# Queries and keys of a hybrid decoder layer moved ahead of attention, as seven block products per pair of heads

## The chip, the cores and the metric

One core of a Trainium2 chip runs the whole layer as one program. The metric is device time in microseconds (us); lower is better. A core has a matrix engine (PE, with its weight loads as PEld), a vector engine (DVE), a scalar engine (ACT), a general engine (POOL) and a queue engine (SP) that issues most transfers. Each takes its own instructions strictly in order.

## The reference

Everything is float32; 1024 tokens, model width 1024, one layer. Cut to what the change touches:

```python
h = rms_norm(x, attn_norm_w)
q, k, v, u, g = jnp.split(h @ w_in, splits, axis=-1)
q = rms_norm(q.reshape(B, S, 8, 2, 64), q_norm_w)      # per head two halves of 64
k = rms_norm(k.reshape(B, S, 8, 2, 64), k_norm_w)
a = diff_attention(q1, q2, k1, k2, v, lam, rel_bias)   # softmax(q1 k1) - lam * softmax(q2 k2), causal
y_a = (rms_norm(a, subln_w) * (1 - lam_init)) @ w_proj_attn
c = causal_depthwise_conv(u_a * sigmoid(u_b), conv_w, conv_b)      # width 31, 1024 channels
y_b = silu(layer_norm(c)) @ w_proj_conv
x = x + (sigmoid(g_a) * y_a + sigmoid(g_b) * y_b) @ w_out
x = x + (silu(gate) * up) @ w_down                     # from rms_norm(x) @ w_gate_up, width 2816
```

## The kernel before, in words

A float32 product is made of three products of rounded parts: each operand is split into a high part (`whi`, cast by ACT, L120) and a low part (`wlo`, a subtraction, on DVE at L125 or on POOL at L131, as the flag `low_by_pool` says), and PE runs high by high, high by low and low by high (L168 to L170).

The program runs in stages, and PE is the engine that nearly always works. After the norm of x and its transposes (`hT`), the values V1, V2 and the first columns of u are made. Then u follows in pairs of column blocks by **seven products** (`u_pair`, `product` at L980): with sums T1 to T4 of the blocks of `hT`, and sums of the weight blocks (`s`, L961 to L964 on POOL), seven block products replace eight. Behind these run the **taps** of the depthwise convolution, 30 for each of eight blocks of 128 channels, each one DVE instruction (L594) on a row of 1024 tokens; the first four blocks' sums lie in PSUM (`CONV_PSUM = 4`), the last four in SBUF. Next come Q0 and V3, and then attention.

**q and k before.** `q_item(h)` multiplies `hT` with the q and k columns of one head, plainly: 192 matmuls of 256 columns. ACT copies the result (L797) and squares it with 16 short instructions per 1024 columns that add up (L800); roots follow, and DVE multiplies them in (L807). Then `turn_qk` turns it: four transposes on PE (`pQ`, L815), a cast by ACT (L822), a low part by DVE (L824), and transfers within SBUF on SP, six for q (L826 to L832) and two for k (L836, L837). Q0 is made before attention, Q1 to Q7 inside it.

**Attention** has 64 steps: eight heads, in each eight tiles of 128 queries in the order 4, 5, 6, 7, 0, 1, 2, 3. A step makes two score rows on PE (`sc`, L1289 with the low keys or queries at L1290), DVE adds the bias and takes the maximum (L1291), ACT takes the exponential (L1296), DVE combines both (L1303 to L1306). One step later the weights are transposed (`pT`, L1328, "turn") and split, and for every second tile multiplied with the values (`pW`, "weigh"), two steps after that turned back. So that PE has work while the others run, each step takes a piece of other products as **fill**: the lists `later` name Q1 to Q7 and the gates G0 to G15 by head, a piece being 48 matmuls of 256 or 24 of 512 columns (5.4 to 5.8 us). Taps left over are handed to DVE by `slack_of`, which gives each step's spare time as two formulas of the tile size. The order of each engine's instructions is set while the program is recorded: a scheduler places them by their dependences and the marks `issue_after`.

**After attention** come y_a, the convolution branch, w_out, and the channel mixer, which the change does not touch.

## Time and profile before

| what | number |
|---|---|
| time, median of 3 runs (lowest to highest) | 1727.1 us (1726.74 to 1728.84) |
| profiled execution: span from first to last instruction | 1725.7 us, 1.4 us under that median |
| instructions | 25863 |
| PE busy | 1714.6 us, 99% of the span |
| DVE, ACT, POOL busy | 1275.4, 862.5, 219.1 us |
| u by seven products (110 to 247) | 137 us |
| Q0 and V3 (247 to 306) | 59 us |
| attention with its fill (306 to 817) | 511 us |

No time of the profiled execution is given beside its span; what lies around it is taken as the 1.4 us by which the median of the runs is longer. In the rows of groups, a line number, an engine, an operation and its tiles come first (`out<-in`), then the count, the busy time, the mean of one in ns, and the idle time of the engine ahead of them with what ended it. In the rows of windows, each engine has busy time and count, then comes the granted clock of PE.

### The profile page before, as it was taken

Reading aid. Unit: us, or ns where it says so; the run is one execution under the profiler, and the core shown is the slowest. Engines: PE = TensorE matmul, PEld = TensorE weight load, DVE = VectorE, ACT = ScalarE, POOL = GpSimd, SP = SyncE. Lnnn points to the kernel's source line nnn. Section 1 sums busy time; section 2 is a strip of 40 time slices with the busy share of each in tenths; the row PEclk is TensorE's granted clock in tenths of the full one; section 3 lists DMA queues with packets and bytes.
Section 4 is the critical chain, followed back from the end, with each engine's and each line's share of the span. In section 5 each row is a group of like instructions: output and inputs, shape, how many; then the busy total and the mean of one; then the engine's idle time right before and its main releaser. Section 6 shows DMA issues by size and latency. Waiting matters only on the chain.

```text
span 1725.7 us, 25863 instructions
## 1 busy us (share of the span) xinstructions
PE 1714.6 (99%) x9243; PEld 1477.9 (86%) x9243; DVE 1275.4 (74%) x2128; ACT 862.5 (50%) x1958; POOL 219.1 (13%) x207
## 2 busy tenths in 40 slices
PE   9999999999999999999999999999999999999999
PEld 7997889998998998988788888888888888888887
DVE  7675889898988888878687769966676666575544
ACT  5333335767777776756556325633333333333332
POOL 3997851000000000000000000000000000000000
PEclk9999999999999999999999999999999999999999
DMA  6344445336345344343973683245455445598663
GB/s 208 116 126 132 131 151 154 104 109 171 104 127 147 115 125 138 101 136 130 333 238 118 200 296 119 74 135 164 147 170 170 154 141 164 175 355 285 217 215 130
DMA packets 261604, 281.64 MB, mean 163 GB/s; under 512 B 16546, under 2 KB 181986, under 8 KB 261475
## 3 DMA queue, kind: packets, MB, share of 16 engines
q1 hardware_dynamic: 254160, 267.71, 48.3%
q0 software_dynamic: 5680, 9.39, 2.6%
q10 hardware_dynamic: 1634, 2.89, 0.5%
q8 instruction: 73, 1.20, 0.3%
q14 instruction: 57, 0.46, 0.1%
HBM read 181.84 MB, written 85.50 MB: 155 GB/s over the span
## 4 chain that ended last, share of the span: by engine, by line
PE 92%; DMA 3%; DVE 2%; ACT 1%; issue 1%; POOL 0%; SPq 0%; DVEq 0%; POOLq 0%; ACTq 0%
PE acc L980 29%; PE acc L488 12%; PE pg L168 12%; PE pg L169 12%; PE pg L170 12%; PE wo L1850 3%; PE sc L1290 2%; PE sc L1289 2%; PE pT L1328 2%; PE pg L1106 1%; DVE acc L594 1%; PE pW L168 1%; PE pW L169 1%; PE pW L170 1%; PE pQ L815 1%
## 5 line engine op out<-in xcount | busy, mean ns | idle before, releaser
L594 DVE SCALAR_TENSOR_TENSOR acc<-u,cw,acc 128x1023 f32<-128x1023 f32 (+14 forms) x240 | 303.4, 1264 | 23.2 <-ACT acc L588 20.7
L170 PE MATMUL pg<-whi,hT_lo 128*128 128x256 f32 x704 | 200.2, 285 | 0.0
L168 PE MATMUL pg<-whi,hT_hi 128*128 128x256 f32 x704 | 199.7, 285 | 0.4 <-DVE v L125 0.4
L169 PE MATMUL pg<-wlo,hT_hi 128*128 128x256 f32 x704 | 199.5, 284 | 0.0
L125 DVE TENSOR_TENSOR wlo<-draw,whi 128x1024 fp32r<-128x1024 f32 x75 | 91.7, 1223 | 83.4 <-ACT whi L120 78.9
L120 ACT CAST whi<-draw 128x1024 fp32r<-128x1024 f32 x75 | 79.1, 1055 | 129.5 <-PE acc L488 114.3
L169 PEld LDWEIGHTS pg<-wlo,hT_hi 128*128 128x128 f32 x704 | 134.4, 191 | 1.8
L170 PEld LDWEIGHTS pg<-whi,hT_lo 128*128 128x128 f32 x704 | 134.3, 191 | 1.8
L168 PEld LDWEIGHTS pg<-whi,hT_hi 128*128 128x128 f32 x704 | 134.0, 191 | 2.1 <-DVE v L125 0.6
L120 ACT CAST whi<-wraw 128x1024 fp32r<-128x1024 f32 x90 | 94.7, 1052 | 70.6 <-PE pg L169 32.6
L488 PE MATMUL acc<-wlo,whi 128*128 128x512 f32 x308 | 119.8, 389 | 0.0
L488 PE MATMUL acc<-whi,wlo 128*128 128x512 f32 x308 | 119.8, 389 | 0.0
L1296 ACT ACTIVATE E<-E,mn 128x640 f32<-128x640 f32 (+7 forms) x128 | 99.8, 781 | 30.8 <-DVE mn L1291 29.2
L168 PE MATMUL pg<-hT_hi,whi 128*128 128x512 f32 x288 | 114.4, 397 | 0.1
L169 PE MATMUL pg<-hT_lo,whi 128*128 128x512 f32 x288 | 113.7, 395 | 0.0
L170 PE MATMUL pg<-hT_hi,wlo 128*128 128x512 f32 x288 | 113.7, 395 | 0.0
L120 ACT CAST whi<-s 128x1024 fp32r<-128x1024 f32 x54 | 56.9, 1053 | 104.9 <-PE acc L980 101.8
L125 DVE TENSOR_TENSOR wlo<-wraw,whi 128x1024 fp32r<-128x1024 f32 x75 | 93.3, 1246 | 12.6 <-ACT whi L120 12.3
L1291 DVE CUSTOM_DVE_ANT_0 E<-sc,tb 128x512 f32<-128x512 f32 (+3 forms) x128 | 74.2, 585 | 33.2 <-PE pT L1328 16.1
L980 PE MATMUL acc<-h_hi,whi 128*128 128x512 f32 x240 | 93.4, 389 | 0.0
L980 PE MATMUL acc<-h_lo,whi 128*128 128x512 f32 x240 | 93.4, 389 | 0.0
L980 PE MATMUL acc<-h_hi,wlo 128*128 128x512 f32 x240 | 90.1, 389 | 0.0
(370 smaller groups left out, 4589.7 us busy)
## 6 DMA issues: line engine op xcount, KB each, us to landing
wraw<-in_w_gate_up_dram SPq DMA_DIRECT2D x44, 512.0 KB, 4.7
wraw<-in_w_in_dram SPq DMA_DIRECT2D x38, 512.0 KB, 4.0
qs<-qs SPq DMA_DIRECT2D x96, 128.0 KB, 2.3
wd<-in_w_down_dram SPq DMA_DIRECT2D x44, 256.0 KB, 3.1
tdT<-wd SPq DMA_DIRECT2D x88, 128.0 KB, 4.8
draw<-sdS SPq DMA_DIRECT2D x44, 256.0 KB, 3.7
draw<-tdT SPq DMA_DIRECT2D x44, 256.0 KB, 3.7
wraw<-in_w_in_dram SPq DMA_DIRECT2D x32, 256.0 KB, 3.3
```

The source lines that it names most:

```text
L120: act.copy(dst, src)
L125: last_lo[0] = dve.tensor_tensor(dst, src, f32(hi), op=ALU.subtract).ins
L168: pe.matmul(o, lh, rh, start=start, stop=False)
L169: pe.matmul(o, lh, rl, start=False, stop=False)
L170: last_mm[0] = pe.matmul(o, ll, rh, start=False, stop=stop).ins
L488: m = pe.matmul(o[s_][i][:], l_[:, ts], r_[:, 512:], start=start and j + y_ == 0, stop=j == n - 1 and y_ == 2, skip_group_check=not start,)
L594: dve.scalar_tensor_tensor(a_, us[c][:, : S - n], cw[:, c, t : t + 1], a_, op0=ALU.mult, op1=ALU.add)
L980: last_mm[0] = pe.matmul(o[:], a_[x_][:, k, :], b_[y_][:, k, :], start=start and k + x_ + y_ == 0, stop=k == 3 and x_ == 1, skip_group_che ...
L1289: pe.matmul(o[:, :w], qh[:, qs], k, start=True, stop=False)
L1291: dve.tensor_tensor_reduce(e[:, ks], o[:, :w], tb[:, S - nk + c0 : S - nk + c0 + w], 1.0, mn[:, j : j + 1] if c0 else 3.0e38, ALU.add, ALU ...
L1296: act.activation(e[:, :nk], e[:, :nk], AF.Exp, bias=mn[:, j : j + 1], scale=-1.0, accum_out=l[:, j : j + 1])
L1850: last_mm[0] = pe.matmul(o[s_][i][:], A[u_], B[v_], start=start and j + y_ == 0, stop=j == 3 and y_ == 2, skip_group_check=not start,).ins
```

## The change

**q and k.** A new stage, `q_stage`, stands between the last u pair and V3. It makes q and k of all eight heads, two heads at a time, by the seven products of `QSEVEN`, with the same token sums T1 to T4 and with sums and differences of the four weight blocks of a pair (`S1` to `S4`). A product is 48 matmuls of 256 columns, a pair 336, all four pairs 1344. The parts of a result are copied (`take`, ACT), added (`plus`, DVE) and, when complete, stored to memory (`qk_d`), squared 512 columns at a time by ACT and summed by a DVE reduction (`keep`). The roots of six heads are taken at once ahead of the last pair, those of the last two before V3 (`qk_roots`, DVE). Weight sums and low parts are POOL's, but for the first pair, where DVE makes two differences, one sum and one low part.

**In attention** nothing of Q is left; q and k are loaded again (`qk_load`, two transfers of 512 KB a head on SP), multiplied with their roots by POOL (`qk_norm`; DVE for head 0) and turned as before, at places named by `free`. The fill is G0 to G15 alone, in pieces of 6 matmuls of 512 columns, one between a step's two score rows (`amid`) and one behind them. A turn is two steps behind its scores instead of one, and values are weighed a step behind the turn. There are six places for score rows (`e_tile`) instead of four. `low_by_pool` stays set through attention, and POOL also multiplies in the norm of the attention output, but for the last head (`subln`).

**Convolution.** Six blocks' sums lie in PSUM, and all but 63 of the items (taps and transfers) of the list are done when attention starts, where 127 were left before. Signs and scales of the norms move into the constants `qn` and `kn`.

```diff
+    wplace = [cycle((1, 2, 0))]
+
     def wtiles():
-        return [wp.tile([P, 1024], F32R, tag=t_, name=nm(t_)) for t_ in ("whi", "wlo")]
+        z = next(wplace[0])
+        return [wp.tile([P, 1024], F32R, tag=f"{t_}{z}", name=nm(t_), bufs=1) for t_ in ("whi", "wlo")]
...
-    last = ["Q0", "V3"]
-    later = [
-        ["Q1", "G0", "G1"],
-        ["Q2", "G2", "G3"],
-        ["Q3", "G4"],
-        ["Q4", "G5", "G6"],
-        ["Q5", "G7"],
-        ["Q6", "G8", "G9"],
-        ["Q7", "G10"],
-        ["G11", "G12", "G13", "G14"],
-        ["G15"],
-    ]
+    last = ["V3"]
+    later = [f"G{c}" for c in range(2 * NKT)]
...
-    CONV_PSUM = 4
+    CONV_PSUM = 6
+    rs = cv.tile([P, 2 * H * 16], F32, tag="rs", name="rs", bufs=1)
...
-            o = gemm_T(w, hT_hi, hT_lo, sb)
+            o = pg()
+            cs = slice(sb * 512, (sb + 1) * 512)
+            for k in range(NKT):
+                mm3(o[:], w[0][:, k, :], w[1][:, k, :], hT_hi[:, k, cs], hT_lo[:, k, cs], k == 0, k == NKT - 1)
+                if k % 2 and k < NKT - 1:
+                    yield
...
+    def qk_load(h, b):
+        raw = qkp.tile([P, 4, 256], F32, tag="qkraw", name=f"qkraw{h}_{b}", bufs=2)
+        nc.sync.dma_start(raw[:].rearrange("p i c -> p (i c)"), qk_d[h][b][:])
+        return raw
+
+    def qk_roots(h0, h1):
+
...
+    def qk_norm(h, b, raw):
+
+        r = rs[:, 32 * h + 16 * b : 32 * h + 16 * b + 16]
+        r4 = raw[:].rearrange("p i (g d) -> p (i g) d", d=HD)
+        (pool if h else dve).tensor_tensor(r4, r4, r.unsqueeze(2).to_broadcast([P, 16, HD]), op=ALU.mult)
+        for z, key in ((1, "k"), (0, "q")):
+            free = NT * (h - 1) + (0 if key == "k" and b else NT - 1 if key == "q" and not b else NT // 2 - 1)
+            late.append((free if h else 0, lambda a_=(h, z, key, b, raw): turn_qk(*a_)))
+
+    def turn_qk(h, z, key, b, raw):
...
+            lo2 = part(4)
+            for one, two in ((s1, s2), (lo, lo2)):
+                if one is lo:
+                    dma(f32(two[HD:, :]), f32(one[HD:, :]))
+                dma(f32(two[:HD, :]), f32(one[HD:, :]))
+                dma(f32(one[HD:, :]), f32(one[:HD, :]))
+            t["q", b] = (s1, lo), (s2, lo2)
...
+    QSEVEN = (
+        ("11", (0, 0), "b"),
+        ("12", (1, 0), "a"),
+        ("S2", 2, "b"),
+        ("S1", 1, "c"),
+        ("S3", 3, "b"),
+        ("S4", (1, 1), "c"),
+        ("22", 4, "b"),
+    )
+    RATE = [3.25]
+    first_q = {}
...
+    def q_pair(c, load):
+
+        B = {(j, l): (hT_hi[:, KH[j], TOK[l]], hT_lo[:, KH[j], TOK[l]]) for j in range(2) for l in range(2)}
+        B.update(TS)
+        tags = ((ps, "pg"), (pg2, "pg2"), (ps, "pm"))
+        o = {}
+        for s_, r in (("b", c), ("a", c + 1), ("c", c + 2)):
+            p_, tag = tags[r % 3]
+            o[s_] = [p_.tile([P, 512], F32, tag=tag, name=nm("qo")) for e in range(2)]
+        seen, out = set(), {}
+        A = dict(first_q) if c == 0 else load.pop("A")
+        raw = load.pop("raw")
+
+        def less(o_, a_, b_, op=ALU.subtract, eng=pool):
...
+            eng.tensor_tensor(o_[:], a_[:], b_[:], op=op)
...
+        def take(k, s_):
+            t_ = quarter(k)
+            for e in range(2):
+                act.copy(t_[:, 2 * e : 2 * e + 2, :].rearrange("p i c -> p (i c)"), o[s_][e][:])
+
+        def plus(k, s_):
+            for e in range(2):
+                t_ = out[k][:, 2 * e : 2 * e + 2, :].rearrange("p i c -> p (i c)")
+                dve.tensor_tensor(t_, o[s_][e][:], t_, op=ALU.add)
+
+        def keep(k):
+            h, b = 2 * c + k[0], k[1]
+            t_ = out[k]
+            nc.sync.dma_start(qk_d[h][b][:], t_[:].rearrange("p i c -> p (i c)"))
+            for e in range(2):
+                jk = wp.tile([P, 512], F32, tag="sg", name=nm("qsq"), bufs=2)
+                act.activation(jk[:], t_[:, 2 * e : 2 * e + 2, :].rearrange("p i c -> p (i c)"), AF.Square)
+                c0 = 32 * h + 16 * b + 8 * e
+                dve.tensor_reduce(
+                    rs[:, c0 : c0 + 8], jk[:].rearrange("p (g d) -> p g d", d=HD), axis=AX.X, op=ALU.add
+                )
+
+        for z, (a_, b_, s_) in enumerate(QSEVEN):
+            hi_lo = A.pop(a_)
+            Bz = B[b_]
+            for i in range(4):
+                ts = slice(i * P, (i + 1) * P)
+                e, w = i // 2, slice(256 * (i % 2), 256 * (i % 2 + 1))
+                for k in range(4):
+                    for x_, y_ in ((0, 0), (0, 1), (1, 0)):
+                        last_mm[0] = pe.matmul(
+                            o[s_][e][:, w], Bz[x_][:, k, ts], hi_lo[y_][:, k, :],
+                            start=s_ not in seen and i % 2 == 0 and k + x_ + y_ == 0, stop=k == 3 and x_ == 1,
+                            skip_group_check=True,
+                        ).ins
+            seen.add(s_)
+            if z == 0:
+                take((0, 0), "b")
+                if c == 0:
+                    less(raw["S1"], raw["21"], raw["22"], ALU.add, dve)
+                    less(raw["21"], raw["11"], raw["21"], eng=dve)
+                less(raw["11"], raw["S1"], raw["11"], eng=pool if c else dve)
+                low_by_pool[0] = c > 0
+                A["S2"] = q_split(raw["11"])
+                low_by_pool[0] = True
+            elif z == 1:
+                plus((0, 0), "a")
+                keep((0, 0))
+                A["S1"] = q_split(raw["S1"])
+            elif z == 2:
+                take((0, 1), "b")
+                A["S3"] = q_split(raw["21"])
+                less(raw["12"], raw["12"], raw["11"])
+            elif z == 3:
+                take((1, 1), "c")
+                A["S4"] = q_split(raw["12"])
+                load(c, "11", "21")
+            elif z == 4:
+                plus((1, 1), "b")
+                keep((1, 1))
+                A["22"] = q_split(raw["22"])
+                load(c, "12", "22")
+            elif z == 5:
+                plus((0, 1), "c")
+                keep((0, 1))
+                load(c, "split 11")
+            else:
+                take((1, 0), "b")
+                keep((1, 0))
+                load(c, "split 12", "sums")
+            yield
...
+        def __call__(self, c, *what):
+            raw, A = self.have.setdefault("raw", {}), self.have.setdefault("A", {})
+            for w in what:
+                if c == H // 2 - 1:
+                    if w[:5] == "split":
+                        ws.ahead = int(w == "split 12")
+                        ws.fetch()
+                elif w == "sums":
+                    raw["S1"] = self.tile("S1")
+                    pool.tensor_tensor(raw["S1"][:], raw["21"][:], raw["22"][:], op=ALU.add)
+                    pool.tensor_tensor(raw["21"][:], raw["11"][:], raw["21"][:], op=ALU.subtract)
+                elif w[:5] == "split":
+                    A[w[6:]] = q_split(raw[w[6:]])
+                else:
+                    raw[w] = self.tile(w)
+                    q_load(raw[w], 2 * (c + 1) + int(w[0] == "2"), int(w[1] == "2"))
...
+    def q_stage():
+
+        with ExitStack() as c_:
+            qs = c_.enter_context(tc.tile_pool(name="qs", bufs=1, side="right", reuse_waits="tile"))
+            load = QLoad(qs)
+            load.have["raw"] = raw = {"11": first_q.pop(0), "12": first_q.pop(1)}
+            raw["S1"] = load.tile("S1")
+            first = load.result()
+            for j, key in enumerate(("21", "22")):
+                raw[key] = load.tile(key)
+                q_load(raw[key], 1, j, nc.scalar)
+            for c in range(H // 2):
+                if c == H // 2 - 1:
+                    with after(last_of(mybir.EngineType.DVE)):
+                        qk_roots(0, H - 2)
+                yield from q_pair(c, load)
...
+        raw = [qk_load(0, b) for b in (1, 0)]
         load_bias(0)
-        ws.ahead = 2
-        yield from run(last[:1])
+        for b in (1, 0):
+            qk_norm(0, b, raw[1 - b])
         bg.until((NKT - CONV_PSUM) * (CW + 1) - 1)
-        yield from run(last[1:])
+        qk_roots(H - 2, H)
+        ws.fetch()
+        yield from run(last)
+        wplace[0] = cycle((0, 1))
...
-    low_by_pool[0] = False
...
+    places = cycle("EEEEwv")
+
+    def e_tile():
+        z = next(places)
+        if z == "E":
+            return aps.tile([P, S], F32, tag="E", name=nm("E"), bufs=4)[:]
+        return f32(wp.tile([P, S], F32R, tag="whi2" if z == "w" else "wlo2", name=nm("Ew"), bufs=1)[:])
...
+            if j == 0:
+                scm.append(last_mm[0])
+                amid()
...
+        eng = pool if h < H - 1 else dve
+        eng.tensor_tensor(an[:], an[:], r.unsqueeze(2).to_broadcast([P, NT, VD]), op=ALU.mult)
...
-                backs.append((n + 2, (h, b, weigh(h, b))))
+                backs.append((n + 1, (h, b, weigh(h, b))))
...
-        return 0 if plan[n // NT] == 6 and n % NT in (4, 6) or n == len(steps) - 1 else 1
+        return 0 if n % NT == 5 and 0 < n // NT < H - 2 or n == len(steps) - 1 else 1
...
+        if h + 1 < H and n % NT in (0, 1):
+            raws[n % NT == 0] = qk_load(h + 1, int(n % NT == 0))
+        if h + 1 < H and n % NT in (1, 2):
+            qk_norm(h + 1, int(n % NT == 1), raws[n % NT == 1])
+        scores(h, i, lambda: more(p))
         scm.append(last_mm[0])
-        more((p + 1) // 2)
-        if n:
-            hp, ip = steps[n - 1]
+        more(p)
+        weigh_ready(n)
+        if n > 1:
+            hp, ip = steps[n - 2]
             turn(hp, ip)
             if ip % 2:
-                weighs.append((n, (hp, ip // 2)))
-        more(p // 2)
+                weighs.append((n + 1, (hp, ip // 2)))
...
```

Three places where the order of instructions moves. **First, PE and DVE at the start of the new stage**, where before PE went on with Q0. Tiles `qo` are sums of products; 2568 and 2569 are slot a (product "12"), 2570 and 2571 slot c (product "S1", whose weights are the split of `qS_261`, that is `whi_2692` and `wlo_2693`). PE:

```order
L1110 MATMUL qo_2569<-whi_2498,hT_lo 128x256
L1110 MATMUL qo_2570<-whi_2692,T1h 128x256
L1110 MATMUL qo_2571<-whi_2692,T1h 128x256
L1110 MATMUL qo_2570<-wlo_2693,T1h 128x256
L1110 MATMUL qo_2570<-whi_2692,T1l 128x256
```

And DVE at the same place; `acc` are taps, `R` a stored result:

```order
L587 SCALAR_TENSOR_TENSOR acc_2422<-u_2075,cw,acc_2422 128x1017
L1088 TENSOR_TENSOR R_2620<-qo_2569,R_2620 128x512
L1074 TENSOR_TENSOR qS_261_2558<-q_263_2560,q_264_2563 128x1024
L1098 TENSOR_REDUCE rs<-qsq_2686 128x8
L587 SCALAR_TENSOR_TENSOR acc_2422<-u_2075,cw,acc_2422 128x1016
L1098 TENSOR_REDUCE rs<-qsq_2689 128x8
```

The sum `qS_261`, from which the third product's weights are split, stands behind the addition that reads the end of the second product.

**Second, POOL in the first heads of attention.** Before, its rows there are fills with zero and transfers:

```order
L1319 MEMSET pl_3608 128x128
L1318 MEMSET ph_3607 128x128
L1319 MEMSET pl_4205 128x128
L776 DMA t_d_316<-b_d 128x1152
L578 DMA cs_d<-c_d_141 512x256
```

Now (`L809` multiplies roots in, `L130` makes a low part, `L1546` is the norm of the output):

```order
L809 TENSOR_TENSOR qkraw_1_4754<-qkraw_1_4754,rs 128x1024
L774 DMA t_d_330<-b_d 128x1152
L130 TENSOR_TENSOR wlo_4771<-wraw_4768,whi_4770 128x1024
L809 TENSOR_TENSOR qkraw_0_4802<-qkraw_0_4802,rs 128x1024
L130 TENSOR_TENSOR wlo_5011<-wraw_5008,whi_5010 128x1024
L1546 TENSOR_TENSOR an_5126<-an_5126,r_5545 128x1024
```

From the first of these to the last row ahead of head 3 there are 13 such operations on whole rows of 1024, where before there are none.

**Third, PE from the turn of the next head's q to its first score**, between heads 5 and 6. Before:

```order
L815 MATMUL pQ_7986<-ident,qkraw_7396 128x128 x4
L168 MATMUL pW_8016<-ph_7873,vh_7504 128x256
L168 MATMUL pg_8281<-whi_7930,hT_hi 128x256
L1289 MATMUL sc_8243<-ks_6_0_8008,qs_6_1_7991 128x512
L1289 MATMUL sc_8247<-ks_6_1_7747,qs_6_1_7991 128x128
L1289 MATMUL sc_8253<-ks_6_0_8009,qs_6_1_7992 128x512
L1290 MATMUL sc_8253<-ks_6_0_8009,qs_6_1_7997 128x512
```

Now:

```order
L821 MATMUL pQ_7894<-ident,qkraw_1_7606 128x128 x4
L168 MATMUL pW_7962<-pl_7794,vh_7789 128x256
L167 MATMUL pg_8275<-hT_hi,whi_7935 128x512
L1469 MATMUL sc_8196<-ks_6_0_7916,qs_6_1_7899 128x512
L1470 MATMUL sc_8196<-ks_6_0_7916,qs_6_1_7902 128x512
L1469 MATMUL sc_8200<-ks_6_1_7813,qs_6_1_7899 128x128
```

(Rows between these, all of the kinds shown, are left out.) The score with the low part of q, `qs_6_1_7902`, now stands directly behind the first one; before, several products stood between.

174 lines of the change are left out of this document (93 added, 81 removed).

## The prediction

> **What bounds the kernel now.** I read the page's engine rows and chain first, then the windows by stage, then the waits of PE.
>
> ```profile
> span 1725.7 us, 25863 instructions
> PE 1714.6 (99%) x9243; PEld 1477.9 (86%) x9243; DVE 1275.4 (74%) x2128; ACT 862.5 (50%) x1958; POOL 219.1 (13%) x207
> PE 92%; DMA 3%; DVE 2%; ACT 1%; issue 1%; POOL 0%; SPq 0%; DVEq 0%; POOLq 0%; ACTq 0%
> ...
> 110.00:247.00 137.00, 136.90 (x611) 111.01 (x610) 104.80 (x98) 52.61 (x71) 103.06 (x67) 1.00 0.42 128
> 247.00:306.00 59.00, 58.64 (x479) 57.91 (x478) 50.68 (x57) 30.86 (x102) 12.69 (x9) 1.00 0.69 189
> 306.00:817.00 511.00, 508.49 (x3394) 464.76 (x3394) 439.13 (x975) 362.26 (x1198) 18.24 (x71) 1.00 0.44 123
> ...
> 322.00:338.00 16.00, 16.00 (x86) 13.65 (x85) 16.00 (x34) 11.07 (x34) 0.00 (x0) 1.00 0.29 83
> 338.00:354.00 16.00, 16.00 (x89) 13.87 (x88) 16.00 (x32) 7.36 (x17) 0.35 (x2) 1.00 0.27 83
> ...
> PE sc L1289 <- DMA ks<-klo: 1.1, 1, 1.1
> PE sc L1290 <- DMA qs<-qs: 0.8, 1, 0.8
> ```
>
> PE is busy 99% of the span and is 92% of the chain, at a granted clock of 1.00. In attention (306 to 817) it lacks 511.00 - 508.49 = 2.5 us, nearly all of it two waits at the start of a head for the transfers that finish k and q. So a matmul that is left out is worth its whole time, as long as what feeds PE keeps up. DVE is the engine to watch: it is busy 439.13 of 511 (86%), and in both windows of 322 to 354 all of the time, while PE loses nothing there. POOL has 18.24 us of work in attention.
>
> **What is saved.** The price of a matmul comes from start to start in the chain, since their busy times overlap.
>
> ```profile
> 44.89 8.63 PE pg L1106 x72
> ...
> 147.85 94.99 PE acc L980 x418
> ```
>
> A matmul of 256 columns takes 8.63 / 72 = 0.120 us, one of 512 takes 94.99 / 418 = 0.227. q and k were 8 heads x 192 = 1536 matmuls of 256; they become 4 pairs x 7 products x 48 = 1344. The 192 fewer save 192 x 0.120 = **23.0 us**. Transposes, scores and gates stay as many. Of the 2.5 us of waits I also take all as gone, since both places are made anew; what stands there now is priced below.
>
> **Moved work.** Of q and k, attention held the matmuls of 256 columns of three lines, of which this is one.
>
> ```profile
> L170 PE MATMUL pg<-whi,hT_lo 128*128 128x256 f32 x423 | 120.9, 286 | 0.0
> ...
> L594 DVE SCALAR_TENSOR_TENSOR acc<-u,cw,acc 128x1023 f32<-128x1023 f32 (+14 forms) x120 | 151.2, 1260 | 2.9 <-ACT acc L588 2.8
> L125 DVE TENSOR_TENSOR wlo<-wraw,whi 128x1024 fp32r<-128x1024 f32 x29 | 35.4, 1219 | 2.8 <-ACT whi L120 2.7
> L1306 DVE SCALAR_TENSOR_TENSOR E<-E,rl,E 128x640 f32<-128x640 f32 (+3 forms) x64 | 52.1, 814 | 0.6
> L807 DVE TENSOR_TENSOR qkraw<-qkraw,r 128x1024 f32<-128x1024 f32 x14 | 17.0, 1218 | 0.0
> L1362 DVE TENSOR_TENSOR an<-an,r 128x1024 f32<-128x1024 f32 x7 | 8.5, 1216 | 0.0
> ...
> L800 ACT ACTIVATE jk<-pg 128x64 f32<-128x64 f32 x220 | 49.8, 226 | 4.8
> L800 ACT ACTIVATION_READ_ACCUMULATOR jk<-pg 128x1 f32 x220 | 43.9, 199 | 0.0
> ```
>
> Without them PE has 511 - 2.5 - 3 x 423 x 0.120 = 356 us there. On DVE, 63 of 120 taps leave attention (at 1.19 from start to start, 75 us), as do the low parts (29 x 1.14 = 33), L807 (16), most roots (7) and L1362 (8): 439 - 139 = 300 of 356 us, 84%, no fuller than before. ACT loses the short squares, 49.8 + 43.9 with their overlap some 76 us, and copies and casts; at about 254 of 356 it is no limit. POOL takes about 36 operations on rows of 1024.
>
> **(a) The start of the new stage: +5.3.** In the order, PE has two products whose weights are ready, and then needs "S1". Its weights are a sum that DVE makes only behind the addition that reads the end of product two; then ACT casts, then POOL makes the low part, and PE has two matmuls to run on the high part alone. The prices:
>
> ```profile
> L1000 DVE TENSOR_TENSOR p<-acc,p 128x512 f32<-128x512 f32 x7 | 4.8, 688 | 1.3 <-PE acc L980 1.1 <-ACT p L998 0.2
> L120 ACT CAST whi<-s 128x1024 fp32r<-128x1024 f32 x54 | 56.9, 1053 | 104.9 <-PE acc L980 101.8
> L131 POOL TENSOR_TENSOR wlo<-s,whi 128x1024 fp32r<-128x1024 f32 x14 | 34.1, 2437 | 10.8 <-ACT whi L120 10.8
> ```
>
> 0.69 + 1.22 (as L125) + 1.05 + 2.44 = 5.4, less two matmuls of 0.12: about 5.2 of waiting, taken as 5.3. No PE work stands in the queue ahead that could cover it. If DVE also comes late to that addition, 8; if product two ends with DVE idle and waits overlap, 4.
>
> In this stall PE would stand for longer than anywhere the profile shows behind the opening, where PEclk stays 1.00 throughout. [...]
>
> **(b) The rest of the q and k stage, and V3: +1.5.** Four pairs are 1344 x 0.120 = 161 us of PE. DVE has 88 taps (105 us), 24 additions and 32 reductions near 0.6 us each (34), four sums and lows (5), roots and the hand-over of blocks (about 10): 154 of 161, close to full but not over, and ACT and POOL have room. Bounds 0 and 6.
>
> **(c) Heads 0 to 2: +7.** In the order head 0 now has 17 taps on DVE in its eight steps. Without taps, roots and what left, DVE has (439 - 143 - 33 - 16 - 8 - 14) / 8 = 28 us a head; with 17 x 1.19, and 1 less for the later turn, that is 47 against 36.7 us of PE rows (120 matmuls of 512, 26 of 256, 8 of 384, 46 of 128): DVE falls 10 us behind by the first score of head 1, and catches up in heads 1 and 2, which have 4 and 6 taps. The same sum for before gives a lag of 6.6 us in the stretch of 322 to 354, where PE lost nothing. So 10 costs 10 - 6.6 = 3.4. But there is POOL:
>
> ```profile
> 271.12 4.77 POOL L131 TENSOR_TENSOR wlo<-wraw,whi 128x1024 fp32r<-128x1024 f32 x2 [17.17 <-ACT whi L120]
> ...
> 270.29 0.17 DVE L656 TENSOR_SCALAR t<-t 128x16 f32<-128x16 f32 x1
> 270.41 1.27 DVE L594 SCALAR_TENSOR_TENSOR acc<-u,cw,acc 128x1010 f32<-128x1010 f32 x1
> 271.60 1.95 DVE L657 TENSOR_TENSOR r<-r,t 128x16 f32<-128x16 f32 x1
> 273.47 1.26 DVE L594 SCALAR_TENSOR_TENSOR acc<-u,cw,acc 128x1009 f32<-128x1009 f32 x1
> 274.65 2.31 DVE L807 TENSOR_TENSOR qkraw<-qkraw,r 128x1024 f32<-128x1024 f32 x1
> 276.88 1.26 DVE L594 SCALAR_TENSOR_TENSOR acc<-u,cw,acc 128x1008 f32<-128x1008 f32 x1
> ```
>
> While POOL makes two low parts back to back, a DVE operation on 16 elements takes 1.95 us instead of 0.17 and ends where POOL's first ends; the next with two operands in SBUF takes 2.31 instead of 1.22. The tap between, whose sum is in PSUM, is not touched. So a DVE instruction with both operands in SBUF is held while POOL works, here (1.78 + 1.09) / 2 = 1.4 us for each POOL operation. In attention the taps left (sums in SBUF) and L1306 are of that kind. With four POOL operations by the end of head 0 the lag is 10 + 5.7 = 16; with 13 by the end of head 2, where it would be 3 ahead, again 16. That costs 16 - 6.6 = 9.4; six places for scores and the later turn may bear more lag. Between 3.4 and 9.4 I take 7, nearer the measured hold; bounds 0 and 22 (below).
>
> [...]
>
> **(d) Where a head begins: +2.5.** The chain before 691.40:
>
> ```profile
> 677.28 0.45 PE pQ L815 x4
> 677.75 0.70 ACT qs L822
> 678.46 0.46 SPq L826
> 678.98 3.23 DMA qs<-qs
> 682.26 0.46 SPq L832
> 682.78 2.58 DMA qs<-qs
> 685.42 5.94 DMA qs<-qs
> 691.40 0.56 PE sc L1290 x2
> ...
> DMA to landing us min/median/max: 2.2/2.3/7.6
> ```
>
> From the turn of q to its last transfer it took 14.1 us; with the last landing in the median 2.3 it would be 10.4. By the order the changed PE has 18.1, 12.8, 11.7, 16.7, 10.4, 7.7 and 10.0 us of work there for heads 1 to 7, and needs the low part with the first score. At 10.0 only head 6 waits, 2.3 us. SP carries two loads of 512 KB a head more. I take 2.5; bounds 0 and 18 (14.1 each time: 1.3 + 2.4 + 3.7 + 6.4 + 4.1).
>
> **(e) The end of attention: +1.5.** Among the last turns and weighings stand 11 matmuls of fill instead of 28 (17 x 0.227 = 3.9 less cover), and the first y_a low part is POOL's, 2.44 instead of 1.22. Bounds 0 and 5.
>
> The other edits (three weight places, one load more of the constants, roots by integers) cost nothing: they lie on DVE and ACT behind 161 us of PE work. Without that cover the roots are about 4 us once.
>
> **Sum**, against the profile's own span: -23.0 - 2.5 + 5.3 + 1.5 + 7 + 2.5 + 1.5 = -7.7, 1718.0 us; with the 1.4 us between span and median, **1719.4**.
>
> **Rivals.** *All but the start is hidden*: -23.0 - 2.5 + 5.3 = -20.2, 1706.9. For it speaks that PE lost nothing at 322 to 354 with DVE full; against it the lag of 10.
>
> *POOL's hold makes attention slower than before*: each of the 13 POOL operations in heads 0 to 2 holds DVE for its full 2.4 us. The lag is then -3 + 31 = 28, less 6.6 gives 22 instead of 7: +7.3, **1734.4**. It decides from about 2.1 us a hold; the trace shows 1.78 and 1.09 where every third DVE row is of that kind, and in head 0 it is also every third (17 taps, 8 of L1306 and 8 small ones of 102), so full holds would be more than what the like mixture shows.
>
> *Transfers at the start of heads eat the gain*: the chain of q takes 12.4 us on average, shortfalls 0.4 + 0.7 + 2.0 + 4.7 + 2.4 = 10.2 instead of 2.5: 0.0, 1727.1, no change. The median landing of 2.3 speaks against it, the 14.1 for it.
>
> **How the numbers follow.** Forecast 0.5, all hidden 0.17, POOL's hold 0.17, transfers 0.16. Predicted 1719.4; its own range, 1712 to 1727, has (c) from 3.4 to 9.4 and (b), (d) and (e) together from 1.5 to 11. Over the cases the range is 1706 to 1735. No change means within 0.2%, 3.5 us, about what a measurement here can tell. Faster: 0.17 + 0.5 x 0.85 + some of the transfers, 0.64; the same 0.18; slower 0.18.
>
> **What would show it.** Right: a gap of 5 us in PE ahead of the third product; attention near 365 us with DVE operations on two SBUF operands longer beside POOL's rows; the q and k stage near 168 us. Wrong: a q and k stage over 175 us (then DVE binds it), waits for `qs` of several us at each head, a granted clock below 1.00, or a change in any stage behind y_a, none of which I expect.

## The result, and the profile after

The changed kernel takes **1770.7 us** (median of 4 runs, 1769.67 to 1772.25) against 1727.0 for the kernel before beside it: a ratio of **1.0254, interval 1.024 to 1.0269**. The forecast was 1719.4, faster. The page's head, the engines and the chain of waits of the changed kernel:

```profile
span 1769.1 us, 25152 instructions
PE 1718.6 (97%) x9051; PEld 1461.8 (83%) x9051; DVE 1290.6 (73%) x2085; ACT 818.6 (46%) x1461; POOL 393.2 (22%) x281
...
PE 82%; DVE 8%; DMA 4%; ACT 2%; issue 2%; POOL 0%; SPq 0%; ACTq 0%; DVEq 0%; POOLq 0%
```

PE's share of the chain falls from 92% to 82%, DVE's rises from 2% to 8%. The windows by stage (length; then busy time and count of PE, PEld, DVE, ACT, POOL; then PE's granted clock) say where:

```profile
242.00:416.00 174.00, 169.09 (x1366) 167.34 (x1366) 156.00 (x163) 71.76 (x97) 103.41 (x45) 0.98 0.42 128
416.00:450.00 34.00, 33.63 (x250) 31.86 (x248) 29.88 (x42) 13.69 (x19) 9.12 (x7) 1.00 0.98 304
450.00:860.00 410.00, 375.96 (x2116) 314.02 (x2116) 327.28 (x793) 267.30 (x692) 92.65 (x103) 0.98 0.52 150
...
860.00:880.00 20.00, 17.63 (x68) 14.14 (x69) 8.48 (x15) 10.39 (x22) 2.51 (x2) 0.83 0.82 291
```

In attention (450 to 860) PE is idle 34 of 410 us and its granted clock is 0.98; before it was idle 2.5 of 511 at 1.00. Its waits, over the whole span (us in total, times, longest):

```profile
PE sc L1469 <- DVE mn L1471: 10.7, 15, 4.3
PE sc L1469 <- DVE pl L124: 3.3, 1, 3.3
PE pS L1553 <- POOL an L1546: 3.1, 1, 3.1
PE qo L1110 <- ACT whi L119: 3.1, 1, 3.1
PE pT L1511 <- DVE pl L124: 3.0, 4, 1.3
...
PE sc L1469 <- DMA ks<-klo: 1.8, 2, 1.3
...
PE qo L1110 <- POOL wlo L130: 1.6, 1, 1.6
```

The largest are scores (`sc`) that wait until DVE has taken the maximum of earlier ones (`mn`), for want of a free place: DVE is late. Before, no wait of PE in attention was longer than 1.1 us.

To compare kernels I take one sum for all: from the first score to the first product of y_a, the length, less PE's own work there (the matmuls recorded, at their price from start to start in the traces: 0.227 us for 512 columns, 0.120 for 256, 0.17 for 384, 0.109 for 128). What remains, **lost**, is idle time, time at a lower clock (0.98 in attention, 1.00 before), and what the ends of matmuls cost where no other follows at once (one of 256 columns is busy for 0.28 us, where the next starts 0.120 behind it). Where a stretch is cut leaves about 1 us of doubt in it. With it the whole difference is laid out:

| part | before | after | difference | by the prediction's terms |
|---|---|---|---|---|
| start to first score | 306.8 | 450.2 | +143.4 | +145.1 |
| attention: PE's own work | 507.8 | 349.1 | -158.7 | -161.3 |
| attention: lost | 8.0 | 61.1 | **+53.1** | +8.5 |
| from y_a on | 903.1 | 908.8 | +5.7 | 0 |
| sum, spans | 1725.7 | 1769.1 | +43.5 | -7.7 |

One line is wrong, and it holds 44.6 of the 51 us between forecast and result. By head, lost is 9.5, 4.7, 11.3, 7.6, 8.0, 6.6, 3.6 and 3.7 us, and about 6 behind the last score; before it was 0.3 to 1.7 in each head. DVE, meanwhile, is busy in every microsecond of head 0, and 73 to 87% of heads 1 to 7.

DVE's instructions in attention (450 to 860), in the changed kernel: taps, the combination of score rows, and a tiny one of one element per partition; then POOL's:

```profile
L587 DVE SCALAR_TENSOR_TENSOR acc<-u,cw,acc 128x1016 f32<-128x1016 f32 (+29 forms) x53 | 81.0, 1527 | 0.1
L1489 DVE SCALAR_TENSOR_TENSOR E<-E,rl,E 128x640 f32<-128x640 f32 (+7 forms) x43 | 36.6, 850 | 0.7
L1487 DVE SCALAR_TENSOR_TENSOR rl<-rl,neglam,l 128x1 f32<-128x1 f32 x64 | 19.7, 312 | 1.1
```

```profile
L130 POOL TENSOR_TENSOR wlo<-wraw,whi 128x1024 fp32r<-128x1024 f32 x14 | 37.6, 2687 | 77.3 <-ACT whi L119 62.6 <-PE pQ L821 14.6
L809 POOL TENSOR_TENSOR qkraw<-qkraw,rs 128x1024 f32<-128x1024 f32 x13 | 25.8, 1985 | 71.1 <-DMA qkraw<-qk_d 62.1 <-PE sc L1470 8.9
L1546 POOL TENSOR_TENSOR an<-an,r 128x1024 f32<-128x1024 f32 x7 | 14.2, 2029 | 8.1 <-DVE r L655 8.1
```

A tap takes 1.53 us on the mean instead of 1.26. POOL works 77.6 us on whole rows.

### The profile page after: what moved, and what is told of

It is laid out like the page before. It is cut to its first block, busy times and chain, and to the rows that moved or that the text cites. A ratio compares the mean times of both kernels' runs of the same rounds, so it can differ in the third digit from the quotient of the medians.

```text
span 1769.1 us, 25152 instructions
## 1 busy us (share of the span) xinstructions
PE 1718.6 (97%) x9051; PEld 1461.8 (83%) x9051; DVE 1290.6 (73%) x2085; ACT 818.6 (46%) x1461; POOL 393.2 (22%) x281
## 4 chain that ended last, share of the span: by engine, by line
PE 82%; DVE 8%; DMA 4%; ACT 2%; issue 2%; POOL 0%; SPq 0%; ACTq 0%; DVEq 0%; POOLq 0%
PE acc L979 29%; PE acc L480 12%; PE qo L1110 8%; PE pg L167 7%; PE pg L168 7%; PE pg L169 7%; PE wo L2048 3%; DVE acc L587 3%; PE sc L1469 1%; PE pg L1280 1%; DMA tb<-t_d 1%; PE sc L1470 1%; DVE E L1471 1%; PE pT L1511 1%; DVE Ew L1471 1%
## 5 line engine op out<-in xcount | busy, mean ns | idle before, releaser
L587 DVE SCALAR_TENSOR_TENSOR acc<-u,cw,acc 128x1023 f32<-128x1023 f32 (+14 forms) x240 | 319.2, 1330 | 23.0 <-ACT acc L581 19.1
L130 POOL TENSOR_TENSOR wlo<-wraw,whi 128x1024 fp32r<-128x1024 f32 x43 | 108.2, 2517 | 123.9 <-ACT whi L119 102.7
L1469 PE MATMUL sc<-ks,qs 128*128 128x512 f32 (+2 forms) x192 | 74.9, 391 | 16.3 <-DVE mn L1471 10.7
L480 PE MATMUL acc<-whi 128*128 128x512 f32 x308 | 84.1, 389 | 0.0
L1476 ACT ACTIVATE E<-E,mn 128x640 f32<-128x640 f32 (+7 forms) x86 | 66.8, 780 | 35.6 <-DVE mn L1471 31.8
L124 DVE TENSOR_TENSOR wlo<-s,whi 128x1024 fp32r<-128x1024 f32 x40 | 49.0, 1225 | 28.2 <-ACT whi L119 28.2
L480 PEld LDWEIGHTS acc<-whi 128*128 128x128 f32 x308 | 57.8, 188 | 12.0
L480 PEld LDWEIGHTS acc<-whi,wlo 128*128 128x128 f32 x308 | 57.8, 188 | 12.0
L480 PEld LDWEIGHTS acc<-wlo,whi 128*128 128x128 f32 x308 | 57.8, 188 | 12.0
L1470 PE MATMUL sc<-ks,qs 128*128 128x512 f32 (+2 forms) x192 | 66.6, 351 | 0.2 <-DMA qs<-qs 0.2
```

The lines of the kernel that those rows point to most:

```text
L124: last_lo[0] = dve.tensor_tensor(dst, src, f32(hi), op=ALU.subtract).ins
L130: pool.tensor_tensor(dst, src, f32(hi), op=ALU.subtract)
L480: m = pe.matmul(o[s_][i][:], l_[:, ts], r_[:, 512:], start=start and j + y_ == 0, stop=j == n - 1 and y_ == 2, skip_group_check=not start,)
L587: dve.scalar_tensor_tensor(a_, us[c][:, : S - n], cw[:, c, t : t + 1], a_, op0=ALU.mult, op1=ALU.add)
L1469: pe.matmul(o[:, :w], qh[:, qs], k, start=True, stop=False)
L1470: last_mm[0] = pe.matmul(o[:, :w], ql[:, qs], k, start=False, stop=True).ins
```

## The experiments

My theory after the result: DVE, slowed by POOL's work on SBUF, is late for PE in all heads, because PE has only 2.7 us of fill a step (768 gate matmuls x 0.227 / 64) where it had 5.2 (with 1344 matmuls of Q x 0.120). Rivals: POOL's results themselves come late; the places of the fill, the later turn or the bias load are at fault; DVE's work matters and fill does not. Each run is a program of its own, and the scheduler orders its engines anew. So a run differs from its kernel by its edit and by the order that comes of it.

**All but a few taps out.**

```diff
+    notaps = [False]
...
-                dve.scalar_tensor_tensor(a_, us[c][:, : S - n], ...)
+                if not notaps[0]:
+                    dve.scalar_tensor_tensor(a_, us[c][:, : S - n], ...)
...
+    notaps[0] = True       # set where attention's recording starts
```

> The changed kernel without the 57 taps that DVE still has in attention (the convolution of the last two blocks stays incomplete; nothing else differs). The changed kernel took 1770.7 us; its attention from the first score to the first product of y_a took 410 us where PE's own work is some 354. Theory DVE: DVE with its taps (81 us, 14 of it holds by POOL) is what PE waits for, so the time falls by 35 to 45 us, to about 1728. Theory thin fill (PE has only 12 fill matmuls a step, and PE, DVE and ACT wait for each other in turn within a step): only head 0, where DVE is full, gains: 8 to 14 us, to about 1758. Theory POOL's hold: taps are half of what is held, 15 to 20 us.

1751.4 us, 19.3 less: not the 35 to 45 of the theory DVE, and more than the 8 to 14 of thin fill. Lost falls to 45.9, but head 0 still loses 11.1: the 16 taps that it runs were recorded earlier and stayed. So the next leaves them out by block:

```diff
+                if c < CONV_PSUM:
                     dve.scalar_tensor_tensor(a_, us[c][:, : S - n], ...)
```

> The changed kernel with the taps of the last two blocks left out altogether (those that were recorded ahead of attention and run in its first head too); POOL as it is. Beside the 1751 without the later taps, the first head gets rid of 16 taps of 1.5 us each (with holds): it lost 9.5 us, so 7 to 12 us more fall, to 1740 to 1744. If the first head's loss is not DVE's, 1748 to 1752.

1736.8, 34 less than the changed kernel and below the forecast of 1740 to 1744; lost 29.3, head 0 down from 9.5 to 2.7. The window of attention:

```profile
450.00:829.00 379.00, 362.99 (x2119) 309.95 (x2119) 258.22 (x741) 268.23 (x693) 88.85 (x104) 1.00 0.55 162
```

DVE's work falls by 69 us and PE's loss by 32; POOL works nearly as long as ever (89 us after 93), and the clock is back at 1.00. So about half of the loss goes with DVE's work.

**POOL's multiplications out.**

```diff
-        (pool if h else dve).tensor_tensor(r4, r4, ...)
+        if h == 0:
+            dve.tensor_tensor(r4, r4, ...)
...
-        eng = pool if h < H - 1 else dve
-        eng.tensor_tensor(an[:], an[:], ...)
+        if h == H - 1:
+            dve.tensor_tensor(an[:], an[:], ...)
```

> The changed kernel without POOL's multiplications in attention (the roots of q and k of heads 1 to 7 and the norm of the output of heads 0 to 6 are left out; their inputs are still loaded and turned): 20 of 34 POOL operations on whole rows are gone, and with them what queued behind them on POOL. Theory POOL's hold: DVE loses 12 of its 21 us of holds and the waits of the output's turn go; the time falls by 12 to 25 us. Theory thin fill: 0 to 6 us.

1750.4, 20 less (its two runs, 1746.7 and 1754.1, lie apart), lost 45.4. That may be the hold or the late results. To tell them apart, POOL does the same work and writes it where nobody reads:

```diff
+            for e in range(2):
+                x_ = wp.tile([P, 512], F32, tag="sg", name=nm("aside"), bufs=2)
+                pool.tensor_tensor(x_[...], r4[:, 8 * e : 8 * e + 8, :], rr, op=ALU.mult)
```

> The changed kernel, with the multiplications that POOL does in attention (the roots into q and k of heads 1 to 7, the norm of the output of heads 0 to 6) reading the same tiles at the same places, but writing their result, in two halves, to a tile that nobody reads. POOL works as long as before, but PE, ACT and the transfers of q and k wait for it no longer; the roots of q and k and that norm are left out of what is computed. Leaving these multiplications out altogether gave 1750.4 instead of 1770.7. Hold theory (POOL's work on SBUF holds DVE, and DVE is what PE waits for): as slow as the changed kernel, 1764 to 1774. Late-result theory (what PE misses is POOL's result, which comes 2 us behind its transfer): 1748 to 1754. Between them, shares of both.

1768.4 (1765.3 and 1771.5), as slow as the changed kernel; lost 60.8. DVE is busy 323 us in attention again, 312 without the multiplications, so POOL's working alone brings holds back. But this run is no pure test. ACT now waits 9.2 us for places that the tiles without readers take; PE's longest stretch without fill holds 12.2 us of its own work, at the prices above, instead of 7.0; and behind the last score 11.9 us are lost, where the changed kernel loses 6.1. The run speaks for the hold, but it doesn't exclude that late results cost a part.

**The same beside the kernel before**, where fill is thick:

```diff
             dve.tensor_tensor(r4, r4, r.unsqueeze(2).to_broadcast([P, 16, HD]), op=ALU.mult)
+            for e in range(4 if h else 0):
+                x_ = wp.tile([P, 512], F32, tag="sg", name=nm("aside"), bufs=2)
+                a_ = raw[:, 2 * (e % 2) : 2 * (e % 2) + 2, :].rearrange("p i c -> p (i c)")
+                nc.gpsimd.tensor_tensor(x_[:], a_, a_, op=ALU.mult)
...
```

> The kernel before, with 35 multiplications of 128x1024 on POOL added in attention, each in two halves, which read a q or k tile or an output tile and write to a tile that nobody reads. Nothing else moves: DVE keeps all its work, PE its fill of 5.5 us a step. Hold theory: DVE, 86% busy there, loses up to 35 x 1.4 = 49 us to holds and goes beyond 95%; PE, which has much fill there, loses 10 to 30 of them: 1737 to 1757. If holds only stretch instructions that nobody waits for: 1726 to 1729.

**1760.3 us**, ratio 1.0195 (1.0166 to 1.0225), above both forecasts, from work whose results nobody reads. First the kernel before: attention by windows, and one group of DVE there. Then this kernel: the same window, and of DVE's groups the combination of score rows (which the prediction shows at 814 ns) and the one of a single element per partition:

```profile
306.00:822.00 516.00, 513.49 (x3417) 468.86 (x3417) 441.57 (x977) 365.38 (x1202) 19.49 (x73) 1.00 0.44 126
```

```profile
L1304 DVE SCALAR_TENSOR_TENSOR rl<-rl,neglam,l 128x1 f32<-128x1 f32 x64 | 13.7, 214 | 0.5
```

```profile
306.00:856.00 550.00, 524.39 (x3416) 473.87 (x3414) 473.42 (x978) 366.90 (x1203) 105.46 (x143) 0.98 0.42 118
```

```profile
L1310 DVE SCALAR_TENSOR_TENSOR E<-E,rl,E 128x640 f32<-128x640 f32 (+3 forms) x64 | 61.7, 965 | 0.9
L1308 DVE SCALAR_TENSOR_TENSOR rl<-rl,neglam,l 128x1 f32<-128x1 f32 x64 | 22.9, 359 | 0.9
```

With the same instructions DVE is busy 32 us longer (473.4 against 441.6), and lost rises by 34 us (from 8.0 to 42.0), though DVE is busy only 86% and PE has 5.2 us of fill a step. That the two sums are close doesn't show that each held microsecond is paid. Matters are worst in head 0. The timelines of POOL, DVE and PE there (start, length; in brackets the idle time before):

```profile
351.01 7.18 POOL L811 TENSOR_TENSOR aside<-qkraw 128x512 f32<-128x512 f32 x4 [9.42 <-DVE rl L1308]
```

```profile
352.23 3.10 DVE L1310 SCALAR_TENSOR_TENSOR E<-E,rl,E 128x1024 f32<-128x1024 f32 x2
355.25 2.04 DVE L594 SCALAR_TENSOR_TENSOR acc<-u,cw,acc 128x1008 f32<-128x1008 f32 x1
```

```profile
354.43 1.94 PE L1332 MATMUL pT<-ident,E 128*128 128x128 f32 x8 [7.06 <-DVE E L1310]
```

While POOL runs from 351.0 to 358.2, DVE's rows lengthen (the tap of 1008 elements takes 2.04 us, where in the kernel before it takes 1.25), and PE, out of fill, stands 7 us for a row that DVE was already late with. But in this program the scheduler has also put PE's fill elsewhere. Of the windows from 338 to 360, here are the instructions on `pg` (the fill) alone, in the kernel before and then in this one (no column for POOL):

```profile
338.00:360.00 22.00, 16.84 (x86) 13.61 (x86) 0.00 (x0) 2.06 (x3) 1.00 0.31 96
```

```profile
338.00:360.00 22.00, 1.04 (x3) 0.98 (x4) 0.00 (x0) 1.36 (x2) 0.65 0.16 48
```

The kernel before has 86 matmuls of fill there, this one 3. From 338.4 to 359.4 PE finds 6.1 us of work and loses the other 14.9, while DVE is only 2.9 us later than before (its tap of 1008 elements starts at 355.25 instead of 352.33). So 14.9 of the 34 us stand at one place that has lost its fill, and the run doesn't tell how they divide between the holds and the new order. That DVE is held is shown by its rows: the combination of score rows takes 965 ns on the mean instead of 814, the row of one element 359 instead of 214. POOL's own zero fills and transfers also stand behind the added work in POOL's order; of waits that POOL ended, PE and DVE show none and ACT 0.9 us at most, but this share is not excluded.

**Low parts alone on POOL, in the kernel before.** (The flag's reset moves from ahead of attention to its end.)

```diff
-    low_by_pool[0] = False
...
+    low_by_pool[0] = False
```

> The kernel before, with the low parts of attention's weights (29) made by POOL instead of DVE, and nothing else: DVE loses 29 x 1.14 = 33 us of work and gains up to 29 x 1.44 = 42 us of holds. Theory thin fill: with 5.5 us of fill a step PE does not feel the holds, 1727 within 4 us. Theory POOL's hold: slower by 8 us or more.

1742.0, ratio 1.0087 (1.0058 to 1.0116): DVE is spared 29 low parts (35.4 us), and still the kernel is 15 us slower, where thin fill allowed 4. In attention DVE is busy 14 us longer (456 against 442), so 29 low parts hold it by about 14 + 35 = 49 us, 1.7 each; lost rises by 12. Here the order has no such gap: PE's longest stretch without fill holds 4.2 us of work, 4.6 before. This is the cleaner case of a hold that PE pays for.

**All of POOL's attention work on DVE.**

```diff
-        (pool if h else dve).tensor_tensor(r4, r4, ...)
+        dve.tensor_tensor(r4, r4, ...)
...
-        eng = pool if h < H - 1 else dve
+        eng = dve
...
+    low_by_pool[0] = False
```

> The changed kernel with all that POOL computes in attention given to DVE (16 low parts, 13 multiplications of q and k, 7 of the output, 1.14 us each: +41 us on DVE, and no holds, -21 us). Theory POOL's hold: the same or up to 10 us faster, since DVE does not wait and latencies shrink. Theory DVE full: 15 to 25 us slower. Theory thin fill: within 8 us either way.

1768.4, 2.4 less, lost 58.5. DVE has 34 instructions more and no whole rows of POOL beside it (without them a tap takes 1.26 us, as the last run with two pairs below shows): an even trade. Then both ends were lightened: no taps of the last two blocks, no multiplications in attention, and the low parts on DVE, so that POOL has no whole rows left there.

```diff
+                if c < CONV_PSUM:
                     dve.scalar_tensor_tensor(a_, us[c][:, : S - n], ...)
...
+        if h == 0:
+            dve.tensor_tensor(r4, r4, ...)
...
+    low_by_pool[0] = False
```

> The changed kernel with the taps of the last two blocks of the convolution left out altogether, POOL's multiplications in attention left out, and the low parts of attention's weights made by DVE: no holds by POOL are left there and DVE has some 75 us less. If DVE's work and its holds are what PE waits for, nearly all of attention's loss goes: 1770.7 - 45 or more, 1725 or less. If the thin fill costs by itself (the chain of a step is longer than what PE has to do meanwhile), 20 us or more stay lost: 1740 to 1750.

1731.8 (1730.9 to 1733.7), ratio 1.0028, lost 27.1: between its two forecasts. That is 5 us below the run without those taps alone (29.3 lost): once they are gone, taking POOL's work away as well brings little.

**Fill.** Each gate matmul done twice, then every second triple:

```diff
-                mm3(o[:], ...)
+                for z in range(2):            # then: range(1 + k % 2)
+                    mm3(o[:], ...)
```

> The changed kernel with each fill product of the gates issued twice (the gates come out doubled): 384 more matmuls of 512 columns, 384 x 2 x 0.227 = 174 us more for PE if nothing hides them (768 are the gates' own; they become 1536). Theory thin fill: the about 55 us that PE now stands in attention are filled, so the time rises by 174 - 50 = about 125 us, to 1895. If PE's waits are at places that fill does not reach (starts of heads, the tail), it rises by 150 or more.

> The changed kernel, with every second triple of the fill's matmuls (the gates) done twice: 384 matmuls of 512 columns more, 87 us of PE work, 1.36 us more in each of the two pieces of a half step; the gates' values are wrong thereby. Doing all twice added 174 us of work and 114.7 us of time, so 60 were hidden. If PE's losses come of having too little work of its own beside DVE: half of the work hides a good half of the losses, 35 to 50 us, so 1808 to 1823. If it took the full doubling (losses come from long single waits of 4 us and more): 10 to 25 hidden, 1833 to 1848.

The first expectation's count is off: 768 matmuls more are run, 174 us. It took 1885.4, 114.7 more, so 60 us of the work were hidden. The second added 87 us and took 1818.0, 47.3 more: 40 hidden. Lost falls from 61.1 to 25.9 with half more, and to 7.1 with the double, the level of the kernel before, while DVE and POOL still do all their work (341 and 93 us busy, against 327 and 93). The window of attention with each gate matmul twice:

```profile
452.00:982.00 530.00, 528.92 (x2888) 453.58 (x2887) 341.23 (x800) 277.82 (x703) 92.63 (x105) 1.00 0.40 116
```

**The places of the fill, the lag, the bias load.** Three edits that a theory of details asked for: both pieces behind the scores and none between them; the turn one step behind again, with four places for scores and three for weights; and, beside that, the bias of the next head loaded four steps ahead.

```diff
-        scores(h, i, lambda: more(p))
+        scores(h, i, lambda: None)
...
-        more(p)
+        more(2 * p)
```

> The changed kernel with both of a step's pieces of fill behind the scores, none between its two score rows. If the place of the fill within the step matters (PE's waits are for score places that DVE frees), 5 to 20 us slower; if it is only the amount, within 4 us of 1770.7.

```diff
-    places = cycle("EEEEwv")
+    places = cycle("E")
...
-        if n > 1:
-            hp, ip = steps[n - 2]
+        if n:
+            hp, ip = steps[n - 1]
...
```

> The changed kernel with the turn one step behind its scores (four places for scores) instead of two (six places), the third weight place used for weights. Theory thin fill: the second step of lag was there to give the chain of a step more time, and without it PE waits more, 10 to 30 us slower than 1770.7. If the lag does nothing: within 5 us.

```diff
-        if n % NT == 0 and h:
-            load_bias(h)
+        if n % NT == 4 and h + 1 < H:
+            load_bias(h + 1)
...
```

> The changed kernel with turns one step behind and four score places (which alone took 1773.1), and one of the two places so freed used to load the next head's bias four steps early instead of at the head's first step. In the profile of the changed kernel the load of the bias takes 8.3 us at the start of head 2 and PE stands 4.5 us behind it, over the heads some 9 us of waits of DVE. If these waits set the start of heads, 6 to 15 us faster than 1773.1; if they are covered by others, within 4 us.

1768.9, 1773.1 and 1775.3: none moves the time by more than 5 us, and none makes it better by more than its runs scatter. None of these details by itself is the cause.

**Part of the fill back.** Three pairs by seven products and two heads of q and k as plain fill in attention; then two pairs and four heads; turn one step behind, five or four blocks' sums in PSUM. Then both again without any whole-row work on POOL in attention, and with the split of "S1" earlier.

```diff
-    later = [f"G{c}" for c in range(2 * NKT)]
+    later = ['G0', 'Q6', 'G1', 'G2', 'Q7', 'G3', ..., 'G15']
+    NP = 3
...
-    CONV_PSUM = 6
+    CONV_PSUM = 5
...
```

> The changed kernel with three pairs of heads in the new stage and q and k of heads 6 and 7 made plainly inside attention, as fill in pieces of 12 matmuls (192 a head, 256 columns), stored and loaded like the others; for its weights a third place is needed, so turns are one step behind with four places for scores, as in the kernel before. The stage shrinks by 336 x 0.120 = 40 us, attention gets 384 x 0.120 = 46 us of PE work. Theory thin fill: nearly all of the 46 us lies where PE stands now, so the time falls by 30 to 40 us, to 1731 to 1741. Theory POOL's hold or DVE full: attention grows by most of the 46 us, 1765 to 1777.

> The same with two pairs in the new stage, and q and k of heads 4 to 7 in attention (92 us of fill, the stage 81 us shorter, 109 taps left for attention). Theory thin fill: some 50 of the 92 us are hidden, then PE is full: 1770.7 - 81 + 92 - 50 = about 1732, little better or worse than one pair. Theory DVE full: the taps that move into attention cost more than the fill gains, over 1750.

```diff
-        (pool if h else dve).tensor_tensor(r4, r4, ...)
+        dve.tensor_tensor(r4, r4, ...)
...
+                    A["S1"] = q_split(raw["S1"])     # first pair: behind its sum
                     less(raw["21"], raw["11"], raw["21"], eng=dve)
...
+    low_by_pool[0] = False
```

> The kernel of h1 (three pairs by seven products ahead of attention, q and k of heads 6 and 7 as plain fill in attention), with nothing left for POOL to compute on whole rows in attention (low parts and multiplications on DVE, as in the kernel before), and with the weights of the product S1 split ahead of those that the stage needs later, so that its start waits less. Against the kernel before: 144 matmuls less (-17.3) and the start of the stage (+3 to +7). If POOL's holds were what h1 lost beyond that: 1718 to 1732, about level with the kernel before. If the thin fill alone is enough to lose it (174 + 46 us of fill in attention instead of 335): 1745 to 1765.

> The kernel of h2 (two pairs by seven products, q and k of heads 4 to 7 as plain fill), with the same two edits: no whole rows on POOL in attention, and the split of S1 earlier. Against the kernel before: 96 matmuls less (-11.5), the start +3 to +7. If POOL's holds were what h2 lost: 1720 to 1732. If thin fill (174 + 92 us) is enough: 1740 to 1755.

1769.2, 1768.5, 1769.2 and 1768.4. None is better than the changed kernel by a measurable amount, and none beats the kernel before. Here my reading of the holds missed: taking them away brought nothing, as on the changed kernel. The runs with three pairs carry an accident besides, as two waits in head 0 of the one without POOL's work show, PE's and then DVE's:

```profile
PE pT L1544 <- DVE E L1522: 12.1, 1, 12.1
```

```profile
DVE neglam L277 <- ACT lsum L276: 5.7, 1, 5.7
```

The head loses 16.8 us. A row of DVE there stands behind `neglam`, and ACT's `lsum` for that stands behind a transfer of tap sums for which ACT waits 9.6 us. PE pays 12.1 us for it (8.2 in the other run of three pairs). That comes of the order, neither of POOL nor of the amount of fill, so these two runs say little of either. Of the last one, attention by windows, and its taps and row combinations:

```profile
381.00:860.00 479.00, 457.14 (x2857) 407.16 (x2858) 409.99 (x947) 296.80 (x731) 18.31 (x72) 0.98 0.51 150
```

```profile
L590 DVE SCALAR_TENSOR_TENSOR acc<-u,cw,acc 128x997 f32<-128x997 f32 (+14 forms) x94 | 118.3, 1259 | 0.0
...
L1522 DVE SCALAR_TENSOR_TENSOR E<-E,rl,E 128x640 f32<-128x640 f32 (+3 forms) x64 | 52.1, 814 | 0.5
```

DVE is busy 410 of 479, 86% as before the change, and nothing is held (1259 and 814 ns, as before). Yet 42 us are lost, where the kernel before loses 8. Put beside each other (fill is 174 us of gates, 174 x 2 or x 1.5, and 23 us for each plain head, over 64 steps):

| kernel | fill a step, us | DVE's share in attention | lost, us |
|---|---|---|---|
| before | 5.2 | 86% | 8 |
| before, POOL's work added | 5.2 | 86% | 42 |
| changed | 2.7 | 80% | 61 |
| changed, fill 1.5 times | 4.1 | 72% | 26 |
| changed, fill twice | 5.4 | 64% | 7 |
| changed, no taps in SBUF | 2.7 | 68% | 29 |
| changed, light DVE | 2.7 | 70% | 27 |
| two pairs, no POOL | 4.2 | 86% | 42 |

DVE's work and PE's fill both set the loss, and DVE's share alone doesn't tell it. Nor does fill a step alone: the second row has as much as the first, but not at the same places, and beside a DVE that is held. **Open** stay the 27 us that the light kernel loses, and why two pairs without POOL lose 42 us: thinner fill is the difference that I can name, but its pieces also stand at other places than before, and no run isolates that.

## Why the prediction was wrong

**The saving (-23.0) and what bounds the kernel**: right. The first score comes 143.4 us later where the terms gave 145.1, and PE's work in attention shrinks by 158.7 of 161.3.

**(a) The start of the stage, +5.3**: right, and a lower clock came on top, for which the sum holds nothing. PE's timeline in the changed kernel:

```profile
259.16 0.28 PE L1110 MATMUL qo<-whi,hT_lo 128*128 128x256 f32 x1
262.50 0.80 PE L1110 MATMUL qo<-whi,T1h 128*128 128x256 f32 x2 [3.06 <-ACT whi L119]
264.93 0.58 PE L1110 MATMUL qo<-wlo,T1h 128*128 128x256 f32 x1 [1.63 <-POOL wlo L130]
265.31 0.41 PE L1110 MATMUL qo<-whi,T1l 128*128 128x256 f32 x1
265.52 0.41 PE L1110 MATMUL qo<-whi,T1h 128*128 128x256 f32 x1
...
268.30 0.31 PE L1110 MATMUL qo<-wlo,T1h 128*128 128x256 f32 x1
268.44 0.28 PE L1110 MATMUL qo<-whi,T1l 128*128 128x256 f32 x1
268.56 0.28 PE L1110 MATMUL qo<-whi,T1h 128*128 128x256 f32 x1
```

The two gaps are 262.50 - 259.16 - 0.12 = 3.2 us and some 2.1 more, 5.3 together: the term, on the path of cast and low part that it named. That it fits to the tenth is luck, as it was rounded up from 5.2. Behind them matmuls start every 0.213 us instead of 0.120 for 3.4 us, and the granted clock is 0.52 from 262.5 to 268.6: 16 x 0.093 = 1.5 us more. The prediction expected no granted clock below 1.00.

**(b) The rest of the stage, +1.5**: near enough. The first score is 1.7 us earlier than the terms gave, but fill has moved across it: 85 matmuls of Q1 (10.2 us) stood ahead of it before, and 36 of the gates (8.2 us) do now. With that, (a), the clock and (b) come to 7.2 us, against 6.8 for (a) and (b).

**(c) Heads 0 to 2, +7**: the step that failed, in size and in place. Heads 0 to 2 lose 25.5 us where they lost 1.7: 23.8, just over its upper bound of 22. And heads 3 to 7, for which it had no term beside the starts of heads, lose 29.5 where they lost 5.2. Two assumptions carried it. First, that a lag of DVE of up to 6.6 us costs nothing, because it had cost nothing before: that room was PE's fill, 5.2 us a step, and the change halves it. That fill is what gives the room is shown by the runs with more of it. Head 0 shows it most simply: DVE was reckoned to fall 10 us behind there, it is busy in all of the head's 46.1 us, and PE, with the 36.7 us of rows that were reckoned, loses 9.5. The lag was right, the free 6.6 were not. Second, "84%, no fuller than before", taken as room outside of heads 0 to 2: the two-pair kernel has the same 86% and loses 42 us. DVE's work itself came to 327 us where 300 were counted, mostly by holds: 53 taps took 81 us, where 57 were counted with 68. POOL's hold was rightly seen, from two rows of the trace, as the risk. In the two runs beside the kernel before, the time grows about as much as DVE's busy time (15 for 14, and 34 for 32, of which 14.9 stand where the fill has gone).

**(d) Starts of heads, +2.5**: right as far as transfers go, as PE's waits for `ks` are 1.8 us. But scores at these places also wait for DVE, and that is in the 24.3 us of heads 3 to 7.

**(e) The end of attention, +1.5**: too small. Behind the last score lost grows by 5.0, and what follows from y_a on takes 5.7 longer, its first 20 us at a clock of 0.83. The upper bound was 5.

**The rivals.** POOL's hold had the sign and the mechanism, for heads 0 to 2 alone and from 2.1 us a hold on; beside the kernel before a multiplication of 1024 holds DVE for 32 / 35 = 0.9 us and a low part for about 1.7, on either side of the 1.4 that the prediction took and less than 2.1. But it happens in all heads, and the room that was to take it up is gone. *All hidden* and *transfers* are out. The range, up to 1735, was too narrow because every bound of (c) was made with the room of the kernel before.

## What to carry to other kernels

When a change takes work away from the engine that binds, ask first what that work was covering: here 161 us of matmuls in attention were what let DVE be late without cost, and without them attention loses 53 us more. An average share of 80 or 86% on an engine that stands in every step's chain says little of room; room is the binding engine's own work per step and where it stands, and it has to be counted anew after the change. And work on POOL was not free here: beside 86 us of it in attention DVE was busy 32 us longer with the same instructions. Try it as work that nobody reads before moving anything there. Where a scheduler orders each program anew, compare the orders before reading such a run: it is the edit and the new order that are measured together.
